# Whole-width products in three of four feed-forward blocks, and a 128-column first product in the latent attention

## The chip, the cores and the metric

The kernel runs on one core of one Trainium2 chip. It is a single launch; inputs and outputs lie in the chip's memory as the reference has them. The metric is the time of one execution in device microseconds (us), the median over runs. The core's engines work from queues of their own, each in its own order, and meet at semaphores: TensorE (PE; its weight loads are shown apart as PEld), VectorE (DVE), ScalarE (ACT), GpSimd (POOL) and SyncE (SP, which here only issues transfers).

## The reference, cut to what matters

Two layers over 512 tokens of width 1024. In each layer three token mixers run side by side (a convolution, a sparse attention and a multi-head latent attention), then a cross attention over 256 memory tokens, then a SwiGLU feed-forward of width 2816. The change touches the latent attention's last product and the first columns of the feed-forward:

```python
def mla_attention(...):                      # 4 heads, 128 queries at a time
    causal = k_idx[None, :] <= (q0 + jnp.arange(ATTN_QBLOCK))[:, None]
    p = jax.nn.softmax(jnp.where(causal, logits, NEG_INF), axis=-1)
    return jnp.einsum('bhqk,bkhd->bqhd', p.astype(v.dtype), v)
...
x = x + memory_cross_attention(rmsnorm(x, norm_xattn[layer]), ...)
gate, up = jnp.split(rmsnorm(x, norm_ffn[layer]) @ w_gate_up[layer], 2, axis=-1)
x = x + (jax.nn.silu(gate) * up) @ w_down[layer]
```

## The kernel before, in words

Every large product is made of three TensorE products. Both operands are split into a high part of a shorter format and the rest (`hilo`, lines 93 and 94: ACT writes the high part, DVE subtracts it from the source and writes the low part), and `mm3` (lines 86, 87 and 88) multiplies high by high, high weight by low activation, and low weight by high activation, into the same accumulator. In the trace these are L86, L87 and L88. Each product has a weight load of its own. `tick`, called by `mm3` after its third product, counts products and now and then lets POOL issue one transfer of a list (`paced`, L449): these prepare sums of weight matrices in memory for later stages.

The program is written in order, and a planner, which has costs for each instruction, puts the instructions of each engine into a fixed order ahead of time: an instruction that is not ready by its reckoning lets a later, ready one pass. On the chip each engine then keeps that order.

*Latent attention.* For each head `head_scores` makes the probabilities of four tiles of 128 queries, and `head_mix` goes through the four tiles of 128 keys from the last (j = 3) to the first (j = 0). For key tile j only the queries from tile j on matter (causal), so the columns are `r = slice(j*128, 512)`: 128 columns for j = 3, 512 for j = 0. The transposed probabilities go to `ph` and `pl`. The accumulator `pvs[h]` (512 queries, one bank of PSUM) must be started by the first product: for j = 3 POOL zeroes the columns 0 to 383 of `ph` (L857), and L864 multiplies all 512 columns. L867 and L868 then take the 128 columns of `r`, and for other j L866, L867 and L868 take `r` alone. One set of products is made between other work: `pump` hands out products of a filler (projections and merges) between the steps of the attention.

*The stage before the feed-forward.* `residual` (L1258 to L1260) multiplies the cross attention's output by `w_xo`, for the four tiles of 128 tokens in turn. After each tile t the sum is added to x (L1272), and `norm_to_hT` makes its RMSNorm: squares on ACT (L210), the factor on DVE and POOL (L198, L201), the scaled rows on DVE (L217), eight 128 by 128 transposes on PE (L225, two banks of four), copies on ACT (L239), and the split into `hTh` (ACT, L93) and `hTl` (DVE, L94), each in two pieces of four blocks of 128 channels (k = 0 to 3, then 4 to 7). `hTh` and `hTl` hold all 512 tokens, tile t in the columns 128t to 128t+127.

*The feed-forward's first pair.* The feed-forward's columns go by pairs of blocks of 128. All pairs but the first use a scheme with seven products over quarters. The first pair is plain: four blocks, two of gate and two of up (lines 1637 to 1650). For each, `fm_blocks` brings the weights (`raw`, two buffers; split into `wh` and `wl`, three buffers each), and `fm_gemm` multiplies them with `hTh` and `hTl` for all eight k, first for the columns 0 to 255 (token tiles 0 and 1), then for 256 to 511 (tiles 2 and 3):

```python
        for i, wu in enumerate(fm_blocks(w_gate_up[l], cols, KD)):
            m = i % 2
            p = bank("mm")
            fm_gemm(p, wu, hx, KD, ((0, 256), (256, 512)))
```

That is 48 products of 256 columns a block, with three accumulator banks of the kind `mm`. A gate block is followed by Silu (L1642), an up block by `keep_act` (L1598). Then the loop over the other pairs begins with its block `gate0` (`product(p1[j][:, q0], u, j, x11)`, followed by the copy L1696). Sums of the token quarters (`token_sums`, L1622 to L1625, with splits named `rh` and `rl`) are made beside this.

## Time and profile before

| | |
|---|---|
| median of 3 runs | 1904.0 us (1902.99 to 1905.19) |
| the profiled execution, first to last instruction | 1903.2 us |
| PE busy | 1878.3 us (99%) |
| DVE busy | 1517.3 us (80%) |
| ACT busy | 1040.2 us (55%) |
| POOL busy | 269.9 us (14%) |
| TensorE clock granted, mean | 0.996 of full |

The time of the profiled execution is its span; what lies around the first and last instruction is not in the trace, and the median of the other runs is 0.8 us above the span. In the rows, times are microseconds from the start of the span. A row of the timeline has the start, the duration, the engine, the line, the operation, output<-input by the program's names, sizes and count; in brackets the idle time of the engine before it, and what ended it. A product's shape is 128*128 (the weights) and 128xN (N columns); because products are pipelined, a row's duration is longer than the distance to the next row, and the distance is what it takes.

### The profile page before, as it was taken

Reading aid. Unit: us, or ns where it says so; the run is one execution under the profiler, and the core shown is the slowest. Engines: PE = TensorE matmul, PEld = TensorE weight load, DVE = VectorE, ACT = ScalarE, POOL = GpSimd, SP = SyncE. Lnnn points to the kernel's source line nnn. Section 1 sums busy time; section 2 is a strip of 40 time slices with the busy share of each in tenths; the row PEclk is TensorE's granted clock in tenths of the full one; section 3 lists DMA queues with packets and bytes.
Section 4 is the critical chain, followed back from the end, with each engine's and each line's share of the span. In section 5 each row is a group of like instructions: output and inputs, shape, how many; then the busy total and the mean of one; then the engine's idle time right before and its main releaser. Section 6 shows DMA issues by size and latency. Waiting matters only on the chain.

```text
span 1903.2 us, 29548 instructions
## 1 busy us (share of the span) xinstructions
PE 1878.3 (99%) x10988; PEld 1645.0 (86%) x10988; DVE 1517.3 (80%) x2787; ACT 1040.2 (55%) x1962; POOL 269.9 (14%) x434
## 2 busy tenths in 40 slices
PE   9999999999999999999999999999999999999997
PEld 8888888888887999998888878888888889999986
DVE  7989898774466899998869999996645678998986
ACT  5376556764345654446544765675534465445563
POOL 1111111111122211100022111111112221110000
PEclk9999999999999999999999999999999999999999
DMA  6666544456876766656567575445566766766664
GB/s 183 153 166 168 161 122 126 122 147 156 230 184 164 183 169 180 192 173 199 182 174 171 156 199 132 123 104 135 159 184 172 219 167 160 196 164 168 202 197 151
DMA packets 217644, 318.52 MB, mean 167 GB/s; under 512 B 16352, under 2 KB 153843, under 8 KB 217500
## 3 DMA queue, kind: packets, MB, share of 16 engines
q1 hardware_dynamic: 183116, 216.39, 36.2%
q0 software_dynamic: 31872, 94.39, 23.9%
q10 hardware_dynamic: 2512, 5.85, 0.8%
q8 instruction: 86, 1.41, 0.3%
q14 instruction: 58, 0.48, 0.1%
HBM read 307.13 MB, written 97.54 MB: 213 GB/s over the span
## 4 chain that ended last, share of the span: by engine, by line
PE 86%; DVE 6%; issue 3%; ACT 2%; DMA 1%; POOL 1%; POOLq 0%; DVEq 0%; ACTq 0%
PE ps_mm L86 14%; PE ps_mm L88 14%; PE ps_mm L87 14%; PE ps_s L86 3%; PE ps_s L88 3%; PE ps_s L87 3%; PE ps_t L86 2%; PE ps_t L88 2%; PE ps_t L87 2%; PE ps_t L1069 2%; PE ps_mm L1359 1%; PE ps_mm L1360 1%; PE ps_mm L1358 1%; PE ps_pv L86 1%; PE ps_pv L88 1%
## 5 line engine op out<-in xcount | busy, mean ns | idle before, releaser
L93 ACT CAST wh<-raw 128x1024 fp32r<-128x1024 f32 (+3 forms) x419 | 422.3, 1011 | 490.3 <-PE ps_mm L87 121.1
L94 DVE TENSOR_TENSOR wl<-raw,wh 128x1024 fp32r<-128x1024 f32 (+3 forms) x419 | 488.5, 1172 | 220.3 <-ACT wh L93 216.5
L86 PE MATMUL ps_mm<-hTh,wh 128*128 128x512 f32 (+1 forms) x1152 | 414.9, 361 | 1.3 <-ACT kraw L551 0.7
L88 PE MATMUL ps_mm<-hTh,wl 128*128 128x512 f32 (+1 forms) x1152 | 411.4, 358 | 0.5 <-DVE wl L94 0.5
L87 PE MATMUL ps_mm<-hTl,wh 128*128 128x512 f32 (+1 forms) x1152 | 411.8, 358 | 0.0
L88 PEld LDWEIGHTS ps_mm<-hTh,wl 128*128 128x128 f32 x1152 | 218.1, 189 | 32.6 <-DVE wl L94 1.3
L86 PEld LDWEIGHTS ps_mm<-hTh,wh 128*128 128x128 f32 x1152 | 218.2, 189 | 30.5 <-issue 1.3
L87 PEld LDWEIGHTS ps_mm<-hTl,wh 128*128 128x128 f32 x1152 | 218.3, 190 | 26.5 <-issue 0.7
L572 DVE SCALAR_TENSOR_TENSOR ca<-u,vT,ca 128x512 f32<-128x512 f32 x240 | 177.4, 747 | 2.9
L449 POOL DMA_DIRECT2D up<-in_w_gate_up_dram x128 | 84.6, 661 | 536.6 <-PE ps_mm L88 396.2
L449 POOL DMA_DIRECT2D down<-in_w_down_dram x132 | 84.8, 642 | 477.1 <-PE ps_mm L88 254.4
L1032 ACT ACTIVATE P<-P,ss 128x512 f32<-128x512 f32 (+3 forms) x128 | 71.3, 558 | 53.7 <-DVE ss L1029 52.7
L93 ACT CAST PTh<-ps_t 128x512 fp32r<-128x512 f32 (+4 forms) x136 | 70.3, 517 | 55.5 <-PE ps_t L1069 45.0
L86 PE MATMUL ps_s<-rh,wh 128*128 128x256 f32 x320 | 90.6, 283 | 0.0
L87 PE MATMUL ps_s<-rl,wh 128*128 128x256 f32 x320 | 90.6, 283 | 0.0
L88 PE MATMUL ps_s<-rh,wl 128*128 128x256 f32 x320 | 90.6, 283 | 0.0
L94 DVE TENSOR_TENSOR PTl<-ps_t,PTh 128x512 fp32r<-128x512 f32 (+2 forms) x120 | 71.5, 597 | 7.8 <-ACT PTh L93 6.6
L1040 ACT ACTIVATE P<-P,sr 128x512 f32<-128x512 f32 (+3 forms) x128 | 63.2, 554 | 17.8 <-DVE sr L1038 17.7
L86 PE MATMUL ps_mm<-op,wh 128*128 128x512 f32 (+1 forms) x192 | 68.8, 359 | 0.0
L88 PE MATMUL ps_mm<-op,wl 128*128 128x512 f32 (+1 forms) x192 | 68.4, 356 | 0.2
L87 PE MATMUL ps_mm<-op,wh 128*128 128x512 f32 (+1 forms) x192 | 68.0, 355 | 0.0
L86 PEld LDWEIGHTS ps_s<-rh,wh 128*128 128x128 f32 x320 | 61.4, 192 | 0.0
(556 smaller groups left out, 4657.8 us busy)
## 6 DMA issues: line engine op xcount, KB each, us to landing
up<-in_w_gate_up_dram POOLq DMA_DIRECT2D x128, 320.0 KB, 4.4
down<-in_w_down_dram POOLq DMA_DIRECT2D x132, 256.0 KB, 4.3
raw<-in_w_in_dram SPq DMA_DIRECT2D x32, 1024.0 KB
raw<-in_w_gate_up_dram SPq DMA_DIRECT2D x60, 512.0 KB
raw<-up SPq DMA_DIRECT2D x40, 512.0 KB
raw<-down SPq DMA_DIRECT2D x40, 512.0 KB
raw<-in_w_down_dram SPq DMA_DIRECT2D x30, 512.0 KB
raw<-in_w_in_dram SPq DMA_DIRECT2D x26, 512.0 KB
```

The costliest lines, as they stand in the source:

```text
L86: nc.tensor.matmul(o, lh, rh, start=start, stop=False)
L87: nc.tensor.matmul(o, lh, rl, start=False, stop=False)
L88: tick(nc.tensor.matmul(o, ll, rh, start=False, stop=stop))
L93: nc.scalar.copy(hi, src)
L94: nc.vector.tensor_tensor(lo, src, f(hi), op=OP.subtract)
L449: d = nc.gpsimd.dma_start(dst, src, accum_op=op) if op else nc.gpsimd.dma_start(dst, src)
L572: nc.vector.scalar_tensor_tensor(c, u[:, j:j + T], cw[:, m, j:j + 1], c, op0=OP.mult, op1=OP.add)
L1032: nc.scalar.activation(p[:, c], p[:, c], AF.Exp, bias=s[:, k:k + 1], scale=-1.0, accum_out=s[:, 4 + k:5 + k])
L1040: nc.scalar.activation(P[k], P[k], AF.Copy, scale=r[:, k:k + 1])
L1069: nc.tensor.transpose(tp[:, w:w + 128], P[k][:, j * 128:(j + 1) * 128], ident)
L1358: nc.tensor.matmul(accs[t], xh, u[0][:, k, :], start=j == 0, stop=False)
L1359: nc.tensor.matmul(accs[t], xh, u[1][:, k, :], start=False, stop=False)
```

## The change

In `head_mix` the memset of `ph` goes, and the first key tile multiplies only its own 128 queries. The product that starts the bank thus writes 128 of 512 columns; the other columns are first written by the later key tiles' products, whose flag says that they don't start a sum. In the feed-forward's first pair only the first block (i = 0) keeps its two halves; the other three multiply all 512 columns at once: 24 products of 512 columns a block in place of 48 of 256. `tick` is called 24 times fewer in each layer.

```diff
                 hilo(ph[:, r], pl[:, r], tp[:, r])
-                if j == NT - 1:
-
-                    nc.gpsimd.memset(f(ph[:, 0:j * 128]), 0.0)
 
                 def products(j=j, r=r, ph=ph, pl=pl):
                     c = slice(h * 128, (h + 1) * 128)
                     vh, vl = Vm[j][0][:, c], Vm[j][1][:, c]
                     if j == NT - 1:
                         pvs[h] = bank("pv")
-                        nc.tensor.matmul(pvs[h], vh, ph, start=True, stop=False)
-                    else:
-                        nc.tensor.matmul(pvs[h][:, r], vh, ph[:, r], start=False, stop=False)
-                    nc.tensor.matmul(pvs[h][:, r], vh, pl[:, r], start=False, stop=False)
-                    nc.tensor.matmul(pvs[h][:, r], vl, ph[:, r], start=False, stop=j == 0)
+                    o = pvs[h][:, r]
+                    nc.tensor.matmul(o, vh, ph[:, r], start=j == NT - 1, stop=False, skip_group_check=True)
+                    nc.tensor.matmul(o, vh, pl[:, r], start=False, stop=False, skip_group_check=True)
+                    nc.tensor.matmul(o, vl, ph[:, r], start=False, stop=j == 0, skip_group_check=True)
...
             p = bank("mm")
-            fm_gemm(p, wu, hx, KD, ((0, 256), (256, 512)))
+            fm_gemm(p, wu, hx, KD, ((0, 256), (256, 512)) if i == 0 else ((0, 512),))
```

## The prediction, made before the change was run

> **What bounds the kernel now.** I read the page first (busy times, the slices, the chain of waits), then the PE's timeline around both edits, then ACT's and DVE's timelines for what the PE's work there needs, and last the windows with the granted clock.

> ```profile
> PE 1878.3 (99%) x10988; PEld 1645.0 (86%) x10988; DVE 1517.3 (80%) x2787; ACT 1040.2 (55%) x1962; POOL 269.9 (14%) x434
> ...
> PE   9999999999999999999999999999999999999997
> ...
> PE 86%; DVE 6%; issue 3%; ACT 2%; DMA 1%; POOL 1%; POOLq 0%; DVEq 0%; ACTq 0%
> ```

> PE is busy 99% of the span and holds 86% of the chain: PE time saved shortens the kernel where PE has other work in hand, and a hole in PE's queue lengthens it one for one. The mean hides what decides here, namely whether such a hole opens at the edit. Two paces first, from PE's timeline:

> ```profile
> 440.00 0.39 PE L87 MATMUL ps_mm<-hTl,wh 128*128 128x512 f32 x1
> ...
> 441.81 0.39 PE L86 MATMUL ps_mm<-op,wh 128*128 128x512 f32 x1
> ...
> 649.11 0.28 PE L86 MATMUL ps_mm<-hTh,wh 128*128 128x256 f32 x1
> ...
> 650.43 0.28 PE L88 MATMUL ps_mm<-hTh,wl 128*128 128x256 f32 x1
> ```

> The first two rows are 8 products apart: 1.81 / 8 = 0.226 us for 512 columns. The last two are 11 apart: 1.32 / 11 = 0.120 us for 256 columns.

> **The change part by part: the latent heads.** In 4 heads of 2 layers one product of 512 columns becomes one of 128.

> ```profile
> 126.85 0.39 PE L864 MATMUL ps_pv<-PTh,op 128*128 128x512 f32 x1
> 127.08 0.22 PE L867 MATMUL ps_pv<-PTl,op 128*128 128x128 f32 x1
> 127.08 0.19 PEld L868 LDWEIGHTS ps_pv<-PTh,op 128*128 128x128 f32 x1
> 127.14 0.27 PE L868 MATMUL ps_pv<-PTh,op 128*128 128x128 f32 x1
> 127.19 0.19 PEld L86 LDWEIGHTS ps_mm<-hTh,wh 128*128 128x128 f32 x1
> ...
> 127.30 0.19 PEld L87 LDWEIGHTS ps_mm<-hTl,wh 128*128 128x128 f32 x1
> ...
> L857 POOL MEMSET PTh<- x8: 417/422/426, 11.2 to 1127.5; 128x384 f32 x8
> ```

> L864 takes 127.08 - 126.85 = 0.23 us. The 128-column products behind it are spaced by their weight loads, which start at 127.08, 127.19 and 127.30: 0.11 us each. So each head saves 0.23 - 0.11 = 0.12 us, and 8 heads 0.96 us: I take 0.9. The bounds: nothing, where PE then waits for the low part that L867 reads (which the longer product covered), and 8 x 0.17 = 1.4 us if the load were hidden and the pace were 0.06 (L867's start to L868's, 127.08 to 127.14). The memset, 0.42 us on POOL, lies on an engine that is 14% busy; I cost its removal at nothing, since the products wait for ACT's and DVE's halves of the same tile as well. If that cover were gone, 8 x 0.42 = 3.4 us would be the most that it gives.

> [...]

> **The three blocks, if PE had always something to do.** 24 pairs a block, 3 blocks, 2 layers: 144 pairs by 14 ns is 2.0 us saved. This alone would be the gain.

> **The three blocks, as they lie.** The halves were not only slower: the first halves need token tiles 0 and 1 only, and PE ran them while tiles 2 and 3 were still being normalised. Layer 0:

> ```profile
> 623.54 0.28 PE L86 MATMUL ps_mm<-hTh,wh 128*128 128x256 f32 x1
> ...
> 627.47 0.28 PE L88 MATMUL ps_mm<-hTh,wl 128*128 128x256 f32 x1
> 627.59 0.28 PE L86 MATMUL ps_mm<-hTh,wh 128*128 128x256 f32 x1
> ...
> 630.24 0.66 PE L225 MATMUL ps_t<-ident,hn 128*128 128x128 f32 x4 [0.20 <-DVE hTl L94]
> ...
> L87 PE MATMUL ps_mm<-hTl,wh 128*128 128x256 f32 x18 | 5.3, 296 | 0.0
> L86 PE MATMUL ps_mm<-hTh,wh 128*128 128x256 f32 x18 | 5.1, 286 | 0.0
> L88 PE MATMUL ps_mm<-hTh,wl 128*128 128x256 f32 x17 | 5.0, 293 | 0.0
> ```

> ```profile
> 628.17 1.42 DVE L217 SCALAR_TENSOR_TENSOR hn<-x,rs,gB 128x512 f32<-128x512 f32 x2 [0.47 <-POOL rs L201]
> 629.50 1.28 DVE L94 TENSOR_TENSOR hTl<-ps_t,hTh 128x512 fp32r<-128x512 f32 x2
> ...
> 631.42 0.59 ACT L93 CAST hTh<-ps_t 128x512 fp32r<-128x512 f32 x1
> ...
> 632.42 0.64 ACT L93 CAST hTh<-ps_t 128x512 fp32r<-128x512 f32 x1
> ...
> 632.43 0.68 DVE L94 TENSOR_TENSOR hTl<-ps_t,hTh 128x512 fp32r<-128x512 f32 x1
> ...
> 633.63 0.68 DVE L94 TENSOR_TENSOR hTl<-ps_t,hTh 128x512 fp32r<-128x512 f32 x1
> ```

> From 623.54 the timeline shows eight triples L86, L87, L88 (two of them parted by the transposes of tile 2); the 24th ends where the next starts, at 627.59: that is block 0's first half. The three group rows are the window 623.5 to 632.4: 53 products. Tile 3's `hTh` comes at 631.42 + 0.59 = 632.01 (k = 0 to 3) and 633.06 (k = 4 to 7), its `hTl` at 633.11 and 634.31. A product on columns 256 to 511 cannot come before. So 53 - 24 = 29 products of that window are first halves of blocks 1 and 2: PE's filling. With whole-width products this filling is gone: blocks 1 to 3 need all four tiles, the loop's `gate0` needs a weight buffer, and the three buffers are held by blocks 0, 1 and 2. I see nothing else that PE could take.

> After the change, then, PE ends block 0's first half at 627.6 and has only tile 3's eight transposes until 632.01. Block 0's first product of the second half goes there, its second (L87) needs `hTl` and starts at 633.1. From it 23 products of 0.120 reach 635.9, and 72 of 0.226 (blocks 1 to 3) reach 652.2. Before, `gate0` starts at 649.11 (quoted above). Block price: 652.2 - 649.1 = 3.1 us lost a layer, the 1.0 us of cheaper products (72 x 14 ns) already in it. Lower bound: the seven other L86 need no `hTl` and could go in the hole, 7 x 0.12 = 0.8 us less; and the tile's chain could end 0.6 us sooner, if its transposes (at 630.24 they wait for a bank that DVE frees, while the scaled rows are ready at 628.17 + 1.42 = 629.6) found a bank free: 1.7 in all. I see no reason for a later chain, as the change adds nothing to ACT or DVE. I take 2.8, nearer to the upper end, since PE's order keeps the triples together. Layer 1 has the same shape:

> ```profile
> 1559.91 0.28 PE L86 MATMUL ps_mm<-hTh,wh 128*128 128x256 f32 x1
> ...
> 1567.48 0.66 PE L225 MATMUL ps_t<-ident,hn 128*128 128x128 f32 x4 [0.18 <-DVE hTl L94]
> ...
> 1569.67 0.68 DVE L94 TENSOR_TENSOR hTl<-ps_t,hTh 128x512 fp32r<-128x512 f32 x1
> ```

> From the first product to tile 3's `hTl` is 9.8 us there and 8.9 us here, so the price is no smaller. Two layers: 5.6 us.

> **The clock.** A hole of 627.6 to 633.1, with 8 short transposes in it, has a second price. This kernel shows it once in its middle, in the windows by microsecond (PE busy, PEld, DVE, ACT, POOL, granted clock, DMA share, GB/s):

> ```profile
> 163.00:164.00 1.00, 0.45 (x2) 0.40 (x3) 0.97 (x3) 0.61 (x3) 0.00 (x0) 1.00 1.08 384
> 164.00:165.00 1.00, 0.40 (x3) 0.03 (x1) 0.97 (x2) 0.86 (x2) 0.00 (x0) 1.00 0.97 345
> 165.00:166.00 1.00, 0.95 (x5) 0.76 (x6) 0.97 (x4) 0.58 (x4) 0.00 (x0) 0.92 0.03 10
> 166.00:167.00 1.00, 1.00 (x4) 0.81 (x3) 1.00 (x4) 1.00 (x3) 0.15 (x1) 0.50 0.00 0
> 167.00:168.00 1.00, 1.00 (x3) 0.76 (x3) 1.00 (x4) 1.00 (x4) 0.36 (x1) 0.50 0.00 0
> 168.00:169.00 1.00, 1.00 (x4) 0.75 (x3) 0.92 (x2) 0.02 (x1) 0.00 (x0) 0.50 0.86 205
> 169.00:170.00 1.00, 1.00 (x7) 0.92 (x6) 0.00 (x0) 0.38 (x1) 0.00 (x0) 0.88 0.30 123
> ```

> After some 3 us of a half idle PE the clock is halved, and 0.08 + 0.50 + 0.50 + 0.50 + 0.12 = 1.70 us of full clock are lost. The new hole is longer and emptier. What falls inside the hole costs nothing, so one halving costs 0 to 1.7 us a layer, depending on where it falls, and a second behind it as much again. I take 1.4, since it can begin only after the hole has lasted and so lies mostly behind it. Two layers: 2.8 us.

> [...]

> **Paced transfers.** 24 products fewer at 0.07 a product are 1.7 steps a layer; the list ends that much later.

> ```profile
> 794.65 0.81 POOL L449 DMA_DIRECT2D down<-down  x1 [4.23 <-DVE wl L94]
> ...
> 869.81 0.34 SPq L1367 DMA_DIRECT2D raw<-down  x1
> ```

> In layer 0 the last step of a list that goes every 5 us or so is at 794.65; 8 us later it is still 65 us ahead of SP's first read of these sums at 869.81, by the second row. I cost it at nothing; were that cover gone, SP's read and the products behind it would wait as long as the step is late, up to 8 us.

> **The sum.** -0.9 + 5.6 + 2.8 = +7.5 us on the profiled 1903.2, that is 1910.7; the median of the runs is 0.8 above that span, so 1911.5.

> **Rivals.**

> *No hole (not slower).* The planner orders DVE and ACT anew so that tiles 2 and 3 are ready when block 0's first half ends. Then only the savings stand: -0.9 - 2.0 = -2.9, 1901.1. The whole of it needs `hTl` of tile 3 at 627.6, 5.5 us sooner; it decides against a loss from about 2.6 us sooner on, since a layer's 3.1 less its 0.45 of the heads is then made up and the hole too short to halve the clock. For it: POOL's factor and the weights' splits stand between the tile's steps (0.47 us of waiting at 628.17). Against it: the order of DVE and ACT is made by what is ready, and nothing that the change takes away was in their way. Chance 0.14.

> *Hole, but the clock holds.* Then -0.9 + 5.6 = +4.7: 1908.7. [...] Against it: the rows at 163 to 170. Chance 0.22.

> *Hole, with the clock halved for two stretches in both layers.* 3.1 a layer and some 2.5 for the clock: -0.9 + 6.2 + 5.0 = +10.3: 1914.3. For it: the hole's 5.5 us are more than one stretch of halved clock (1.70 / 0.5 = 3.4 us). Against it: once PE runs again, one stretch was enough at 169. Chance 0.10.

> **How the numbers follow.** My forecast has 0.54. A measurement of this kernel tells 0.2%, 3.8 us, from no change: slower is above 1907.8, faster below 1900.2. The forecast lies above the first bound but for its low end (from -0.9 + 3.4 + 0 = +2.5 to -0.9 + 6.2 + 3.4 = +8.7, its own range 1906.5 to 1912.7), the second rival just above it, the third well above: slower 0.74. Same gets most of the no-hole case, part of the second rival and the forecast's low end: 0.20. Faster needs the no-hole case with the memset's gain too: 0.06. The range leaves out the no-hole case and the far end: 1904.5 to 1914.5.

> **What would show it.** Right: in layer 0, PE idle before L225 and before L86 or L87 of `ps_mm` between 627 and 633, ended by DVE's `hTl`, 4 to 5 us in all, the same in layer 1; granted clock 0.50 for 3.4 us just behind; 144 products fewer of 256 columns; L864's line with 128 columns and loads 0.11 apart. Wrong: PE without a gap there, so that something else fills it; or tile 3's `hTl` ready 3 us sooner; or the clock at 1.00 throughout; or a difference far from these two places, which would mean that the planner's order moved elsewhere.

## The result, and the profile after

The changed kernel takes 1919.25 us (median of 5 runs, 1916.37 to 1920.48) where the kernel before, on the same chip, takes 1903.17 (median of 5, 1902.98 to 1905.19): a ratio of 1.0076 [1.0065, 1.0087], slower by 0.8%. (The ratio is not the quotient of the two medians, which is 1.0084 here; the two can differ by a tenth of a per cent.) The forecast was slower by 0.4%, 1911.5, with a range to 1914.5. The profiled execution has a span of 1918.8 us, 15.6 above the one of before, and a mean granted clock of 0.991 instead of 0.996.

The page after, at the places shown of before (busy times, PE's slices, the chain by engine):

```profile
PE 1884.3 (98%) x10844; PEld 1643.5 (86%) x10844; DVE 1517.9 (79%) x2787; ACT 1040.5 (54%) x1962; POOL 267.5 (14%) x426
...
PE   9999999999999999999999999999999999999997
...
PE 84%; DVE 6%; issue 4%; DMA 3%; ACT 2%; POOL 1%; POOLq 0%; DVEq 0%; ACTq 0%; SPq 0%
```

PE has 144 products fewer and yet is busy 6 us longer: products at a halved clock take longer (for 256 columns 0.21 us instead of 0.12, below). Its slices still show nines throughout, and the chain says hardly more, 2% of it having gone from PE to DMA and issue; the loss lies in pieces that only windows and waits show. The first is in the first pair (PE's timeline of after):

```profile
622.59 0.28 PE L86 MATMUL ps_mm<-hTh,wh 128*128 128x256 f32 x1
...
626.51 0.28 PE L88 MATMUL ps_mm<-hTh,wl 128*128 128x256 f32 x1
629.29 1.97 PE L225 MATMUL ps_t<-ident,hn 128*128 128x128 f32 x8 [2.50 <-DVE hTl L94]
631.57 1.44 PE L86 MATMUL ps_mm<-hTh,wh 128*128 128x256 f32 x3 [0.31 <-ACT hTh L93]
632.80 0.41 PE L87 MATMUL ps_mm<-hTl,wh 128*128 128x256 f32 x1
633.01 0.42 PE L88 MATMUL ps_mm<-hTh,wl 128*128 128x256 f32 x1
...
652.89 0.28 PE L86 MATMUL ps_mm<-hTh,wh 128*128 128x256 f32 x1
```

Block 0's first half ends at 626.6, and then PE has nothing for 2.50 us, the transposes of tile 3, and three high products until 632.8. From the first product to `gate0` it is 652.89 - 622.59 = 30.30 us, where before has 649.11 - 623.54 = 25.57: 4.7 lost. The granted clock stands in the windows of after (PE busy, PEld, DVE, ACT, POOL, clock, DMA share, GB/s):

```profile
628.00:629.00 1.00, 0.00 (x0) 0.00 (x0) 1.00 (x2) 0.27 (x1) 0.00 (x0) 1.00 0.85 233
629.00:630.00 1.00, 0.71 (x4) 0.71 (x5) 1.00 (x3) 0.00 (x0) 0.00 (x0) 0.63 1.00 305
...
635.00:636.00 1.00, 1.00 (x6) 1.00 (x6) 1.00 (x3) 0.00 (x0) 0.29 (x1) 0.50 0.03 2
636.00:637.00 1.00, 1.00 (x10) 1.00 (x10) 0.56 (x1) 0.00 (x0) 0.00 (x0) 0.96 0.94 82
```

It is halved from 629.3 to 636.1, 6.8 us. The products of 256 columns are 0.21 us apart there instead of 0.12 (632.80 to 633.01). Layer 1 has the same hole:

```profile
1570.70 0.28 PE L86 MATMUL ps_mm<-hTh,wh 128*128 128x256 f32 x1
...
1578.81 1.97 PE L225 MATMUL ps_t<-ident,hn 128*128 128x128 f32 x8 [3.91 <-DVE hTl L94]
...
1602.14 0.28 PE L86 MATMUL ps_mm<-hTh,wh 128*128 128x256 f32 x1
```

That is 31.44 us, where before `gate0` starts at 1586.34:

```profile
1586.34 0.28 PE L86 MATMUL ps_mm<-hTh,wh 128*128 128x256 f32 x1
```

so 1586.34 - 1559.91 = 26.43, and 5.0 are lost. Together the pair costs 9.7 of the 15.6 us. To see where the rest lies, the same ACT and DVE instructions were paired in both traces, and the median difference of their starts taken in stretches: -0.5 before 190, -1.0 in 400 to 600, +3.8 in 660 to 1040, +6.7 at 1105, +9.8 in 1140 to 1200, +10.9 in 1330 to 1450, +10.4 ahead of layer 1's first pair, +15.8 behind it and to the end. So 6 to 7 us go in the mixers of layer 1, between 1040 and 1330, where the change edits only one product of each head, and makes it shorter. The windows of 90 us there, of before and then of after:

```profile
1050.00:1140.00 90.00, 87.80 (x476) 73.93 (x475) 83.53 (x177) 61.53 (x128) 11.16 (x22) 1.00 0.66 180
```

```profile
1050.00:1140.00 90.00, 84.79 (x433) 70.37 (x433) 77.88 (x156) 58.46 (x119) 9.27 (x18) 0.96 0.63 164
```

PE is empty 3.0 us more, and the clock, 1.00 before, has a mean of 0.96. In this stretch ACT waits longer for its weights. What ACT waits for from 1045 to 1135 (us in total, times, longest), of before and then of after:

```profile
ACT w L93 <- DMA raw<-in_cmp_w_k_dram: 0.6, 1, 0.6
ACT w L93 <- DMA raw<-in_cmp_w_v_dram: 0.3, 1, 0.3
```

```profile
ACT w L93 <- DMA raw<-in_cmp_w_k_dram: 3.9, 2, 2.1
ACT w L93 <- DMA raw<-in_cmp_w_v_dram: 2.5, 2, 1.5
```

Two theories, then. **T1**: the loss is that of the first pair (hole and clock) plus a second thing: `tick`'s counter `paced["due"]` is not set back between the layers, so that 24 groups fewer at 0.07 let layer 1's list begin with another rest (0.02 before; 0.02 - 1.68 + 2 = 0.34 after), and its transfers go at other places. **T2**: it is the heads' edit, through the planner's order or its products, that costs in layer 1.

### The profile page after: what moved, and what is told of

Its sections match the earlier page's. It is cut to its first block, busy times and chain, and to the rows that moved or that the text cites. A ratio compares the mean times of both kernels' runs of the same rounds, so it can differ in the third digit from the quotient of the medians.

```text
span 1918.8 us, 29244 instructions
## 1 busy us (share of the span) xinstructions
PE 1884.3 (98%) x10844; PEld 1643.5 (86%) x10844; DVE 1517.9 (79%) x2787; ACT 1040.5 (54%) x1962; POOL 267.5 (14%) x426
## 2 busy tenths in 40 slices
PE   9999999999999999999999999999999999999997
## 4 chain that ended last, share of the span: by engine, by line
PE 84%; DVE 6%; issue 4%; DMA 3%; ACT 2%; POOL 1%; POOLq 0%; DVEq 0%; ACTq 0%; SPq 0%
PE ps_mm L86 14%; PE ps_mm L88 14%; PE ps_mm L87 14%; PE ps_s L86 3%; PE ps_s L88 2%; PE ps_s L87 2%; PE ps_t L86 2%; PE ps_t L88 2%; PE ps_t L87 2%; PE ps_t L1065 2%; PE ps_mm L1355 1%; PE ps_mm L1356 1%; PE ps_mm L1354 1%; PE ps_pv L86 1%; PE ps_pv L88 1%
## 5 line engine op out<-in xcount | busy, mean ns | idle before, releaser
L93 ACT CAST wh<-raw 128x1024 fp32r<-128x1024 f32 (+3 forms) x419 | 422.4, 1011 | 502.7 <-PE ps_mm L87 124.3
L94 DVE TENSOR_TENSOR wl<-raw,wh 128x1024 fp32r<-128x1024 f32 (+3 forms) x419 | 488.3, 1171 | 220.9 <-ACT wh L93 212.2
L86 PE MATMUL ps_mm<-hTh,wh 128*128 128x512 f32 (+1 forms) x1104 | 409.6, 372 | 2.1 <-ACT kraw L551 0.7
L87 PE MATMUL ps_mm<-hTl,wh 128*128 128x512 f32 (+1 forms) x1104 | 405.6, 367 | 0.0
L88 PE MATMUL ps_mm<-hTh,wl 128*128 128x512 f32 (+1 forms) x1104 | 404.8, 367 | 0.4 <-DVE wl L94 0.4
L88 PEld LDWEIGHTS ps_mm<-hTh,wl 128*128 128x128 f32 x1104 | 210.7, 191 | 34.8 <-DVE wl L94 1.2
L86 PEld LDWEIGHTS ps_mm<-hTh,wh 128*128 128x128 f32 x1104 | 210.8, 191 | 34.0 <-ACT hTh L93 1.4
L87 PEld LDWEIGHTS ps_mm<-hTl,wh 128*128 128x128 f32 x1104 | 210.9, 191 | 28.9 <-issue 0.7
L449 POOL DMA_DIRECT2D up<-in_w_gate_up_dram x128 | 85.0, 664 | 562.8 <-PE ps_mm L88 459.9
L449 POOL DMA_DIRECT2D down<-in_w_down_dram x132 | 85.0, 644 | 494.2 <-PE ps_mm L88 228.9
L93 ACT CAST PTh<-ps_t 128x512 fp32r<-128x512 f32 (+4 forms) x136 | 70.4, 518 | 54.0 <-PE ps_t L1065 43.4
L86 PE MATMUL ps_s<-rh,wh 128*128 128x256 f32 x320 | 90.6, 283 | 0.0
L87 PE MATMUL ps_s<-rl,wh 128*128 128x256 f32 x320 | 90.6, 283 | 0.0
L88 PE MATMUL ps_s<-rh,wl 128*128 128x256 f32 x320 | 90.6, 283 | 0.0
L94 DVE TENSOR_TENSOR PTl<-ps_t,PTh 128x512 fp32r<-128x512 f32 (+2 forms) x120 | 71.4, 597 | 9.6 <-ACT PTh L93 9.0
L86 PE MATMUL ps_mm<-op,wh 128*128 128x512 f32 (+1 forms) x192 | 68.7, 358 | 0.0
L88 PE MATMUL ps_mm<-op,wl 128*128 128x512 f32 (+1 forms) x192 | 68.5, 357 | 0.2
L87 PE MATMUL ps_mm<-op,wh 128*128 128x512 f32 (+1 forms) x192 | 68.1, 355 | 0.0
L86 PEld LDWEIGHTS ps_s<-rh,wh 128*128 128x128 f32 x320 | 61.4, 192 | 0.0
```

The costliest lines, as they stand in the source:

```text
L86: nc.tensor.matmul(o, lh, rh, start=start, stop=False)
L87: nc.tensor.matmul(o, lh, rl, start=False, stop=False)
L88: tick(nc.tensor.matmul(o, ll, rh, start=False, stop=stop))
L93: nc.scalar.copy(hi, src)
L94: nc.vector.tensor_tensor(lo, src, f(hi), op=OP.subtract)
L449: d = nc.gpsimd.dma_start(dst, src, accum_op=op) if op else nc.gpsimd.dma_start(dst, src)
```

## The experiments

**The heads alone.** The edit of `head_mix` as in the change; all four blocks keep their halves.

> The heads' part alone; all four feed-forward blocks keep their halves. Both theories: 0.9 to 1.0 us faster than before (8 products of 512 columns become 128), about 1902.2; PE's order is otherwise that of before. A loss here would mean that the heads' part feeds the disturbance in layer 1.

Measured: 1903.88 against 1904.76; ratio 0.9996 [0.9987, 1.0004]. Nothing is lost in layer 1 (the shift is -1.6 at 1040 and -1.0 at 1140 to 1450). T2 falls. The saving forecast, 0.9 us, is 0.05% and too small to be told: the interval holds it, and it holds no change as well.

**The counter alone.** The kernel before, with the counter set back as the change does it, and no product changed:

```diff
             fm_gemm(p, wu, hx, KD, ((0, 256), (256, 512)))
+            paced["due"] -= 8 * paced["rate"] * (i > 0)
```

> The kernel before, with the products of before, but the counter of the paced transfers set back by 24 products' worth in each layer (1.68 steps), as the change does by having fewer products. Theory A (the hole in PE's queue and the halved clock behind it are all): nothing changes, 1903.2. Theory B (the counter's rest is carried into layer 1, where the paced transfers then fall on other weight transfers and cost about 6 us between 1050 and 1130 and 1 us near 1260): 4 to 7 us slower, 1907 to 1910, with ACT waiting for raw transfers in layer 1's latent attention.

Measured: 1911.88 against 1904.76; ratio 1.0033 [1.0022, 1.0044]. That is theory B, with a median a little above its range; theory A falls. All of the work is that of before. The shift stays within 0.3 us of nothing up to 1040, is +1.9 at 1105, +6.0 in 1140 to 1200, and +7.7 at the end. The waits of ACT are those of after:

```profile
ACT w L93 <- DMA raw<-in_cmp_w_k_dram: 3.2, 2, 1.9
ACT w L93 <- DMA raw<-in_cmp_w_v_dram: 2.9, 2, 1.5
```

and at a place where PE waits already before, it waits more. PE's timeline of before, and then of this kernel:

```profile
1102.66 0.50 PE L866 MATMUL ps_pv<-PTh,op 128*128 128x512 f32 x1 [0.15 <-ACT PTh L93]
1104.20 0.50 PE L867 MATMUL ps_pv<-PTl,op 128*128 128x512 f32 x1 [1.04 <-DVE PTl L94]
...
1105.71 0.33 PE L700 MATMUL ps_mm<-ident,h 62*128 62x62 f32 x2 [0.66 <-DVE h L696]
```

```profile
1104.52 0.50 PE L866 MATMUL ps_pv<-PTh,op 128*128 128x512 f32 x1 [1.48 <-ACT PTh L93]
1106.07 0.50 PE L867 MATMUL ps_pv<-PTl,op 128*128 128x512 f32 x1 [1.05 <-DVE PTl L94]
...
1107.57 0.47 PE L700 MATMUL ps_mm<-ident,h 62*128 62x62 f32 x2 [0.66 <-DVE h L696]
```

PE waits 1.3 us longer for ACT's `PTh`, three waits in a row leave PE mostly empty for some 4.5 us, and behind them this kernel's windows show

```profile
1107.00:1114.00 7.00, 6.43 (x18) 5.25 (x19) 4.87 (x14) 4.17 (x10) 0.00 (x0) 0.51 0.08 28
```

7 us at half clock, where before has 1.00 in each of these. The products run from 1108 to 1114 at half pace: some 3 us of the 7.7 by which this trace is behind at its end. Some 2 us had been lost in waits by 1105, and 1.3 come in 1235 to 1330. How much of the clock's part the counter causes can't be read from single traces: of the eleven kernels profiled here the clock is halved from a point between 1105.0 and 1110.6 on in eight, and four of these eight (the next four experiments) have the counter of before.

**The change without the counter's effect.** The whole change, and the counter gets back what the 24 groups would have added:

```diff
             fm_gemm(p, wu, hx, KD, ((0, 256), (256, 512)) if i == 0 else ((0, 512),))
+            paced["due"] += 8 * paced["rate"] * (i > 0)
```

> The whole change, but the counter gets what the missing products would have added, so the paced transfers keep their places. Theory A: as the changed kernel, 1919. Theory B: only the holes remain, 2 x 4.7 us, less 0.9 of the heads: 1911 to 1912.

Measured: 1913.80; ratio 1.0039 [1.0026, 1.0052], which is 7.4 us (9.0 by the medians). With the 0.0033 of the counter alone this makes 0.0072, and the change had 0.0076 [0.0065, 0.0087]; by the medians 9.0 + 7.1 = 16.1, and the change had 16.1. Within these intervals the two parts account for the whole. The time lies nearer to theory B (1911 to 1912) than to A (1919). The shift is +3.6 from 660 to 1068 and +3.5 at 1105, and then +5.1 in 1140 to 1200: the clock is halved for 3.4 us from 1110.0 on here too. The pair costs 652.70 - 623.09 - 25.57 = 4.0 us in layer 0 and 1597.03 - 1565.60 - 26.43 = 5.0 in layer 1 (PE's timeline):

```profile
623.09 0.28 PE L86 MATMUL ps_mm<-hTh,wh 128*128 128x256 f32 x1
...
652.70 0.28 PE L86 MATMUL ps_mm<-hTh,wh 128*128 128x256 f32 x1
...
1565.60 0.28 PE L86 MATMUL ps_mm<-hTh,wh 128*128 128x256 f32 x1
...
1597.03 0.28 PE L86 MATMUL ps_mm<-hTh,wh 128*128 128x256 f32 x1
```

**The hole filled with work that nobody needs.** The same, and block 0 has 32 products of 256 columns between its halves, into a bank that nobody reads. Where PE would wait it multiplies; the hole's length stays. If it is the empty stretch that halves the clock, the clock should hold.

```diff
+            if i == 0:
+                fm_gemm(p, wu, hx, KD, ((0, 256),))
+                spare = bank("s", "spare")
+                for n in range(32):
+                    nc.tensor.matmul(spare[:, 0:256], wu[0][:, n % KD, :], hTh[:, n % KD, 0:256], start=n == 0, stop=n == 31)
+                fm_gemm(p, wu, hx, KD, ((256, 512),))
+            else:
+                fm_gemm(p, wu, hx, KD)
+            paced["due"] += 8 * paced["rate"] * (i > 0)
```

> As e6_due, and in block 0, between its halves, PE also makes 32 products of 256 columns into a spare bank that nobody reads: they fill the hole without being of use. If the halved clock costs about 1.5 us a layer, this is 3 us faster than e6_due (1908 to 1909), with the clock at 1.00 there; if the clock costs nothing, it is as e6_due or a little slower.

Measured: 1911.15; ratio 1.0032 [1.0021, 1.0043]. Its PE timeline, and its windows at the former hole:

```profile
621.46 0.28 PE L86 MATMUL ps_mm<-hTh,wh 128*128 128x256 f32 x1
...
625.53 2.32 PE L1639 MATMUL spare<-hTh,wh 128*128 128x256 f32 x18
628.17 0.66 PE L225 MATMUL ps_t<-ident,hn 128*128 128x128 f32 x4 [0.32 <-DVE hTl L94]
...
649.89 0.28 PE L86 MATMUL ps_mm<-hTh,wh 128*128 128x256 f32 x1
...
1565.54 0.28 PE L86 MATMUL ps_mm<-hTh,wh 128*128 128x256 f32 x1
...
1594.83 0.28 PE L86 MATMUL ps_mm<-hTh,wh 128*128 128x256 f32 x1
```

```profile
629.30:633.00 3.70, 3.70 (x31) 3.57 (x30) 3.70 (x7) 2.31 (x7) 0.69 (x1) 1.00 0.66 248
633.00:638.00 5.00, 5.00 (x28) 4.32 (x27) 5.00 (x8) 4.34 (x6) 0.21 (x1) 1.00 0.46 60
```

The clock holds (1.00 in both windows, where the change has 0.50 and 0.69), and tile 3's transposes come as long after the first product as in the change (628.17 - 621.46 = 6.71 us, there 629.29 - 622.59 = 6.70). The pair costs 28.43 - 25.57 = 2.86 us in layer 0 and 29.29 - 26.43 = 2.86 in layer 1. That is the hole by itself; what the kernels with an empty hole lose beyond it, 1.2 and 2.1 (counter given back) or 1.9 and 2.1 (the change), is put down to the clock, as nothing else in the pair differs but the filling. By the medians the filling gains 1913.80 - 1911.15 = 2.7 us (forecast 3, at 1908 to 1909), by the ratios 1.3, with intervals that overlap: the times alone would not have shown it.

**Fewer blocks at full width.** The heads, the counter given back, and only the last block (`i < 3` keeps halves), or the last two (`i < 2`), at full width. The first:

> The heads' part, and whole-width products in the fourth block alone: blocks 0, 1 and 2 keep their halves, and the paced counter gets what the missing products would have added. The fourth block's weights wait for a buffer of block 0, so it never filled the hole: no hole, no moved transfers, 2 x 24 pairs by 14 ns = 0.7 us and the heads' 0.9 saved, 1901.6 beside 1903.2 (or 1.6 below whatever the kernel before takes beside it). If whole-width products were slower in themselves, it would be slower than before.

Measured: 1905.82 against 1904.40; ratio 1.0007 [0.9998, 1.0016]. The gain forecast, 1.6 us or 0.08%, lies outside this interval, so something costs about as much again; the one place that its trace shows is named below. And the second:

> As e8_last with whole-width products in blocks 2 and 3; blocks 0 and 1 keep halves. Block 1's first half (24 products, 2.9 us) stays as filling, 12 products or so of block 2 are lost: a hole of about 1.4 us a layer, too short to halve the clock, less 48 pairs by 14 ns = 0.7: +0.7 a layer, less the heads' 0.9: about +0.5, 1903 to 1904.5. If any hole halves the clock: 3 us more.

Measured: 1905.52; ratio 1.0005 [0.9996, 1.0014]. Neither can be told from before by its time. In the traces the pair costs -0.3 us with one block (in both layers, by the paired instructions), and with two 648.56 - 622.65 - 25.57 = +0.34 in layer 0 by PE's rows, and no clock falls there (1.00 in all its windows from 622 to 650):

```profile
622.65 0.28 PE L86 MATMUL ps_mm<-hTh,wh 128*128 128x256 f32 x1
...
629.34 0.66 PE L225 MATMUL ps_t<-ident,hn 128*128 128x128 f32 x4 [0.19 <-DVE hTl L94]
...
648.56 0.28 PE L86 MATMUL ps_mm<-hTh,wh 128*128 128x256 f32 x1
```

Two blocks' first halves are 48 products, 5.8 us, and nearly reach tile 3 (PE waits 0.6 us there); one block's 24 leave the hole. The first of these kernels also speaks against too simple a reading of layer 1: its counter and the order of its DVE and ACT are those of before, and yet the profiled run, the slowest of its eleven (1901.13 to 1910.60), loses 7 us between 1068 and 1200, with ACT waiting for the same weights and PE behind it:

```profile
ACT w L93 <- DMA raw<-in_cmp_w_v_dram: 3.5, 1, 3.5
```

```profile
1123.13 0.36 PE L682 MATMUL ps_mm<-w,xt 128*128 128x256 f32 x1 [2.74 <-ACT w L93]
```

Its clock is halved there for two stretches of 3.4 us, from 1106.8 and from 1123.9 on. So this stretch is a weak place that can break without any move of the transfers.

**Other rests of the counter.** If another place for the transfers is what costs, other rests must show it. In the kernel before, where layer 1's list begins:

```diff
             paced["issued"], paced["rate"] = 0, 0.0
+            paced["due"] = (paced["due"] + 0.66) % 1.0
```

and the same with 0.15 and 0.85: rests of 0.68, 0.17 and 0.87. At 0.17 a group, one group is some 0.7 us. In POOL's timelines the transfer that before issues at 1056.56 is issued at 1054.05 with the rest of 0.34; with 0.68 the one nearest to that place is issued at 1059.06.

> The kernel before; only the counter of the paced transfers is set 0.66 of a step further where layer 1's list begins (the change sets it 0.32 further). If the loss in layer 1 comes from where the transfers fall, it is another than e7_shift's 7 us: somewhere between 2 us faster and 4 us slower than before (1901 to 1907). If any change of place costs, or the planner's other order in that layer as such, it is again about 1910. The layers up to 1040 us stay as before.

> The kernel before, with the rest of the transfers' counter set from 0.02 to 0.17 where the list of the second layer begins; nothing is left out of the computation. At the rate of 0.17 a group of three products this lets most of that layer's transfers go one group earlier, about half a microsecond. Theory A (the place that the transfers have in the kernel before is one that happens to fit, and every other one costs): 4 to 8 us slower, 1908 to 1912, as with the rests of 0.34 and 0.68. Theory B (the cost grows with the distance from that place): under 3 us slower, 1904 to 1907. Theory C (only luck of the clock's windows, not the transfers): within 2 us of before.

> The kernel before, with the rest of the transfers' counter set from 0.02 to 0.87 where the list of the second layer begins; nothing is left out of the computation. At the rate of 0.17 a group of three products a rest of 0.87 lets the first transfer go five groups sooner, which is one group later than the place before of the transfer ahead of it: the places are those of the kernel before, one group later, and one transfer further in the list. Theory A (every other place costs): 4 to 8 us slower, 1908 to 1912. Theory B (the cost goes by the distance from the nearest place of before): under 3 us slower, 1904 to 1907. Theory C (only the clock's windows): within 2 us of before.

| rest at the start of layer 1 | ratio to before | |
|---|---|---|
| 0.02 (before) | 1 | |
| 0.17 | 1.0006 [0.9998, 1.0015] | 1905.27 against 1904.37 |
| 0.87 | 1.0020 [1.0011, 1.0029] | 1908.12 against 1904.37 |
| 0.34 (as in the change) | 1.0033 [1.0022, 1.0044] | 1911.88 against 1904.76 |
| 0.68 | 1.0044 [1.0031, 1.0057] | 1912.46 against 1904.40 |

Each ratio is to before on the same chip; 0.17 and 0.87 ran on one chip, 0.34 and 0.68 on two others. By these points the cost grows with the distance from the place before: nothing that can be told one group sooner (0.17), 0.20% one group later (0.87, where the next transfer of the list stands five groups sooner), 0.33% two sooner (0.34), 0.44% two later (0.68, four sooner). That every other place costs alike does not hold, nor that only the clock's luck is at work. Two forecasts missed: 0.68 was to lie between 1901 and 1907 if the place of the transfers is what costs (1912.46 is nearer to its other branch, about 1910, if any change of place or order does), and 0.87, with 3.8 us, lies between theory B (under 3) and theory A (4 to 8). The instructions are the same in all five; what the source changes is when POOL issues, and the planner's order follows behind 1235, in one stretch or two. At 0.17 it differs from that of before as well (from 1252 to 1288), and nothing is lost, so another order as such is not what costs. At 0.68 the waits for these weights hardly grow:

```profile
ACT w L93 <- DMA raw<-in_cmp_w_k_dram: 0.8, 1, 0.8
ACT w L93 <- DMA raw<-in_cmp_w_v_dram: 0.6, 1, 0.6
```

and the loss is spread over the layer (1.0 to 1.9 us at each of five places from 1040 to 1620, one of them with the clock halved from 1107.3 on). It is therefore not one collision that costs, and which transfer hits which wait in each case was not followed up; it stays open.

## Why the prediction was right, and where it failed

The measured 1919.25 lies above the upper end of the range, 1914.5. The hole and the clock came about as forecast; the step that failed is the paced transfers, which the prediction put at nothing.

*The hole.* Predicted 2.8 us a layer (between 1.7 and 3.1), with PE idle from 627.6 until tile 3's `hTh` and `hTl`. Measured, with the clock held, 2.86 and 2.86. The rows stand where the prediction put them: the wait ends with DVE's `hTl` (2.50 and 3.91 us), and the second half's first `hTl` product starts at 632.80 - 622.59 = 10.2 us after the first product (predicted 633.1 - 623.5 = 9.6; the three products ahead of it ran at half clock). Of the 4 to 5 us of idle PE that were to show, 2.8 (2.50 and 0.31) and 4.2 do: at the halved clock the transposes and the three products ahead stretch over the rest. The rival without a hole, 0.14, is out. The 14 ns by which its block price has two halves dearer than a whole are 2 x 0.120 - 0.226, from the two paces of before; the whole products of the change go at 0.227 us too (643.37 to 649.49, 27 products).

*The clock.* Predicted 1.4 a layer within 0 to 1.7; measured 1.2 to 2.1. The sign was right and the rival that lets the clock hold is out; the size was a little low, since in three of the four holes of the two kernels the clock was halved for two stretches and not one (6.8 us from 629.3; part of it falls inside the hole and costs nothing). In layer 0 the longest empty stretch of PE was 2.50 us, and the clock fell, at 629.26, before the first of tile 3's eight transposes started, at 629.29; in layer 1 it was 3.91. One case speaks for transposes counting as work of PE for the clock, the kernel with the counter given back, in two stretches of 3.41 us ahead of its hole's halved clock:

```profile
625.31:628.72 3.41, 1.98 (x16) 1.59 (x14) 2.94 (x6) 3.41 (x7) 1.41 (x1) 1.00 0.83 275
628.72:632.13 3.41, 1.78 (x11) 1.25 (x11) 3.41 (x6) 1.69 (x6) 0.00 (x0) 1.00 1.00 324
```

Eight transposes of tile 2 lie in the first; without them PE would be busy there for 1.4 us and not 1.98, less than the 1.72 us behind which the clock of before fell at 165.8, and yet here it held behind the first and fell only behind the second, with 1.78. This is one case.

*The heads.* Predicted -0.9 for the eight heads of both layers. The first key tile's three products are now three of 128 columns, 0.11 apart by their loads, as predicted (PE's timeline of after):

```profile
126.64 0.19 PEld L863 LDWEIGHTS ps_pv<-PTl,op 128*128 128x128 f32 x1
...
126.75 0.19 PEld L864 LDWEIGHTS ps_pv<-PTh,op 128*128 128x128 f32 x1
...
126.86 0.19 PEld L86 LDWEIGHTS ps_mm<-hTh,wh 128*128 128x128 f32 x1
```

The saving itself was not measured. In the trace of after, PE begins layer 0's first pair 623.54 - 622.59 = 0.95 us sooner, with four heads behind it (0.5 by the prediction), but the kernel with the rest of 0.17, which is that of before up to there, is 2.8 us ahead by then in its profiled run. The times of the heads alone can't resolve it, nor a gain from the memset.

*These three steps together.* The sum was +7.5. The kernel with just them (the change with the counter given back) has +7.4 by its ratio and +9.0 by the medians. The interval goes from 5.0 to 9.9 us, so that the agreement to 0.1 us is luck; that the hole and the clock have about the right size is not, as the traces show each of them.

*Paced transfers: the step that failed.* The prediction asked what 24 groups fewer do to the end of layer 0's list, and costed that at nothing. For layer 0 this holds: with the counter alone, nothing moves by more than 0.3 us up to 1040. It did not ask where the counter stands when the next list begins. It isn't set back, layer 1's transfers go two groups sooner, and that costs 6.3 us (0.33%, between 4.2 and 8.4) by itself. Some 3 us of it in the trace are a clock that falls at a place where before holds it; since it falls there in four kernels with the counter of before too, the times show what the counter costs, and how that divides into waits and clock stays open. The sum should have been 7.5 + 6.3 = 13.8, so 1917.8; the change has 1919.25. The prediction had named the sign of it among what would prove it wrong, "a difference far from these two places", but the planner's order was not the first cause: up to 1235 the instructions of PE, DVE and ACT in layer 1 stand in the order of before, and +5.8 of the shift (3.8 to 9.6) has come by then. Behind it the order differs, and 1.3 more come in 1235 to 1330; whether by the order was not tried.

*The rival with two halved stretches* (1914.3, 0.10) had the clock's stretches right and, for want of the transfers, the time still 5 us too low.

## What to carry to other kernels

Before making products wider, ask what the narrow ones were covering: a cheaper instruction that must wait for more inputs can open a hole, and here the hole on PE was paid twice: 2.86 us a layer in its length, and 1.2 to 2.1 in the clock behind it. When an edit changes how often a counter is stepped, follow the counter to every place where it is read, across the loop over layers too, and not just to the end of the list at hand. In a kernel with PE at 99%, a place where PE waits three times in a row is a weak place: here the clock fell behind it when transfers had moved by some 2.5 us, and in some executions with no such move.

## What the runs showed of the hardware beside this

Ahead of the end of the span, before has two stretches of halved clock, from 12.24 and 165.84 on, each 3.413 us long in the trace's own record of the clock. The change has five, from 11.45, 165.05, 629.26, 1110.54 and 1578.16 on, the first two of 3.413 us and the others of 6.827. Their starts are 153.60, 464.21, 481.28 and 467.63 us apart: 45, 136, 141 and 137 times 3.413, to within 0.05. So in each of the two executions they lie on one grid. Divided into pieces at this grid, from 20 us on and without the end, the two traces agree on more. The full clock was halved behind a piece with PE busy for 50% of the time in before (1.72 of 3.41 us, from 162.42 on), and in the change behind pieces with 50% (161.63), 28% (625.85), 35% (1107.13) and 4% (1574.75). Behind all others it held; the emptiest of them had 65% (2.21 of 3.41 us, before, from 1101.09 on). The halved clock stayed for another piece where PE had been busy for 90, 86 and 72% of the one at hand (the change, from 629.26, 1110.54 and 1578.16 on), and came back where it had been for 100%. These are the shares of two traces and no limit: with the rest of 0.87 a piece of 50%, from 1258.6 on, was without consequence (clock 1.00 from 1225 to 1335).
